# Gathered rows, cumulative sums and a projection: four pairs of tiles stored together, and shorter leads

## The chip, the core and the metric

The kernel runs on one core of a Trainium2 chip. The metric is the device time of one execution in microseconds. The kernel before took 454.2 us in the median of six runs (452.15 to 456.44).

## The reference

For each of 16 batches, 2048 rows of 512 fp32 numbers are picked by sorted indices out of 4096, summed up cumulatively along the rows, and multiplied by a 512 x 512 matrix:

```python
# x: (16, 4096, 512) f32, indices: (16, 2048) i64, w: (512, 512) f32
gathered = x[b_idx, indices, :]
cs = np.cumsum(gathered, axis=1)
return np.matmul(cs, w).astype(np.float32)        # (16, 2048, 512)
```

So 67 MB are read by rows and 67 MB are written.

## The kernel before

The rows are cut into tiles of 128, 16 tiles for a batch and T = 256 in all, and two tiles make a pair (R = 2, G = 128 pairs). Each tile goes through these steps, one function for each, with its line in the profile:

- `gather` (L137, POOL): an indirect DMA brings 128 rows of 2 KB into a buffer `g32`. There are 16 such places (NG), so gather t waits on `s_c` until tile t-16, with its pair, has been cast.
- `cast` (L152, ScalarE): fp32 to fp16, from `g32` to `g16`; where the lead allows, a pair is cast in one instruction of 1024 elements.
- `sums` (L164, PE): four matmuls by a triangle of ones give the cumulative sums within the tile, transposed, into one of four PSUM tiles `pa` (NA).
- `carry` (L196, and L183 for the first tile of a batch, VectorE): adds the last column of the tile before, and writes fp16 `cst`.
- `project` (L208, PE): four matmuls of `cst` with the fp16 weights, into one of four PSUM tiles `pb` (NB).
- `drain` (L220, ScalarE): copies `pb` to a buffer `ob` in SBUF. There are 8 buffers (NO), each holding a pair.
- `store` (L234, SP): one DMA of 512 KB for each pair, 128 partitions of 4 KB, once both tiles of the pair are drained. The first and the last pair (`PLAIN`, L229) are stored as two transfers of 256 KB. Before `ob` is written again, ScalarE waits on `s_o` for the store of eight pairs earlier.

Every engine's order is written out by hand, with semaphores between the engines. ScalarE does, for each u from 0 to 255, the casts listed in `casts[u]` and then the drain of u (`step`). That list lets casts run ahead of the drain by `far` tiles, at most FAR = 10; the lead grows from 2 at the start and shrinks at the end:

```python
far = min(FAR, 2 + u // 4, 2 + (T - 1 - u) // 4)
n = R if far > 4 and len(cast_by) % R == 0 else 1
lead = min(LEAD, 1 + (u + 2) // 4, 1 + (T - 1 - u) // 6)
```

PE's order is made likewise from `lead`: sums run ahead of the projection by at most LEAD = 4 tiles. Inside `sums` and `project` a wait for the next step's buffer stands between the matmuls. PE, VectorE and ScalarE run the middle of their orders as hardware loops over 16 tiles (U); POOL and SP have theirs written out.

Of the kernel before, what the change touches and what calls it, by code (L numbers as in the profile page):

```python
# [7 lines left out]
P = 128  # L8
FP32 = mybir.dt.float32
# [24 lines left out]
def kernel(  # L34
# [7 lines left out]
    nc = tc.nc  # L42

    B, S, D = x.shape
    N = indices.shape[1]
    R = 2
# [3 lines left out]
    T = B * NT  # L50
    G = T // R
# [1 line left out]
    KI = T // P  # L53
    FIRST = 2 * R
    NG = 16
    LEAD = 4
    FAR = 10
    NH = 8
    NA = 4
    NB = 4  # L60
    NC = 4
    NO = 8
    U = NT
    assert U % NG == 0 and U % (R * NO) == 0 and U % NA == 0 and U % (R * NC) == 0 and U % NB == 0
    assert D == 512 and N % (R * P) == 0 and T % P == 0

    x_flat = x.rearrange("b s d -> (b s) d")
# [1 line left out]
    const = ctx.enter_context(tc.tile_pool(name="const", bufs=1))  # L69
# [13 lines left out]
    g32 = [const.tile([P, R, D], FP32, name=f"g32_{i}") for i in range(NG // R)]  # L83
    g16 = [const.tile([P, R, D], FP16, name=f"g16_{i}") for i in range(NH)]
    cst = [const.tile([P, DC, R, P], FP16, name=f"cst{i}") for i in range(NC)]
    ob = [const.tile([P, R, D], FP32, name=f"ob{i}") for i in range(NO)]
    pa = [ps.tile([P, DC, R, Q], FP32, name=f"pa{i}") for i in range(NA)]
    pb = [ps.tile([P, D], FP32, name=f"pb{i}") for i in range(NB)]

# [2 lines left out]
    def sem(name):  # L92
        return tc.alloc_semaphore(name)

    s_z, s_ut, s_wc, s_if, s_pt, s_prep, s_of, s_c = (
        sem(f"s_{n}") for n in ("z", "ut", "wc", "if", "pt", "prep", "of", "c")
    )
    s_first = [sem(f"s_first{k}") for k in range(2)]
    s_w = [sem(f"s_w{c}") for c in range(DC)]
    s_idx = [sem(f"s_idx{k}") for k in range(KI)]  # L100
    s_el = [sem(f"s_el{j}") for j in range(R)]
    s_ol = [sem(f"s_ol{j}") for j in range(R)]
    s_g = [sem(f"s_g{i}") for i in range(NG)]
    s_o = [sem(f"s_o{i}") for i in range(NO)]
    s_a = sem("s_a")
    s_d = sem("s_d")
    s_b = sem("s_b")
    s_e = sem("s_e")

    pool, pe, dve, act, sp = (  # L110
        Lane(e) for e in (nc.gpsimd, nc.tensor, nc.vector, nc.scalar, nc.sync)
    )

    casts = []
    cast_by = []
    for u in range(T):
        far = min(FAR, 2 + u // 4, 2 + (T - 1 - u) // 4)
        casts.append([])
        while len(cast_by) <= min(u + far, T - 1):
            n = R if far > 4 and len(cast_by) % R == 0 else 1  # L120
            casts[u].append((len(cast_by), n))
            cast_by += [cast_by[-1] + 1 if cast_by else 1] * n

    for u in range(3 * U, T - 2 * U):
        assert casts[u] == [(t + U, n) for t, n in casts[u - U]]

    def gather(t):
# [20 lines left out]
    def cast(t, n, first=None):  # L148
        g, r = divmod(t, R)
        for u in range(t, t + n):  # L150
            act.need(s_g[u % NG], 16 * (u // NG + 1), first)
        nc.scalar.copy(  # L152
            out=g16[g % NH][:, r : r + n], in_=g32[g % (NG // R)][:, r : r + n]
        ).then_inc(s_c, 1)
# [62 lines left out]
    def drain(u, first=None):  # L217
        g, j = divmod(u, R)
        act.need(s_b, u + 1, first)
        nc.scalar.copy(out=ob[g % NO][:, j], in_=pb[u % NB][:]).then_inc(s_e, 1)  # L220

    def store(g):
        b, h = divmod(g, GB)
        rows = out[b, h * R * P : (h + 1) * R * P, :]
        if g in PLAIN:
            for j in range(R):
                sp.need(s_e, R * g + j + 1)
                done = s_ol[j] if g else (s_o[0], s_of)[j]
                nc.sync.dma_start(  # L229
                    out=rows[j * P : (j + 1) * P, :], in_=ob[g % NO][:, j]  # L230
                ).then_inc(done, 16)
            return
        sp.need(s_e, R * (g + 1))
        nc.sync.dma_start(  # L234
            out=rows.rearrange("(p j) d -> p j d", j=R), in_=ob[g % NO][:]
        ).then_inc(s_o[g % NO], 16)


    with nc.allow_non_contiguous_dma(reason="a few indices, one per partition"):
        for k, eng in enumerate((nc.sync, nc.scalar)):  # L240
            t = k * R
            eng.dma_start(  # L242
                out=idx_first[:, t : t + R, :],
                in_=indices[0, t * P : (t + R) * P]
# [4 lines left out]
    for k in range(KI):  # L249
        nc.sync.dma_start(  # L250
            out=idx64[:, k, :], in_=idx_rows[k * P : (k + 1) * P, :]
        ).then_inc(s_idx[k], 16)
    for c in range(DC):
        eng = (nc.sync, nc.scalar)[c % 2]
        eng.dma_start(out=w32[:, c, :], in_=w[c * P : (c + 1) * P, :]).then_inc(s_w[c], 16)
    for g in range(G):
        store(g)
    for g in range(G - NO, G - 1):
        sp.need(s_o[g % NO], 16 * (g // NO + 1))
    for j in range(R):  # L260
        sp.need(s_ol[j], 16)


    nc.gpsimd.memset(ident[:], 1.0).then_inc(s_ut, 1)
# [3 lines left out]
        out=ident[:],  # L268
        in_=ident[:],
# [7 lines left out]
        out=ut[:],  # L277
        in_=ut[:],
# [9 lines left out]
        out=uq[:],  # L288
        in_=uq[:],
# [23 lines left out]
    for k in range(KI):  # L313
# [3 lines left out]
            out=pb[k % NB][:, :P], in_=idxf[:, k, :], identity=ident[:]  # L317
# [20 lines left out]
    order = []  # L338
    done = 0
    for u in range(T):  # L340
        lead = min(LEAD, 1 + (u + 2) // 4, 1 + (T - 1 - u) // 6)
        first = u if u // R in PLAIN else u // R * R + R - 1
        while done < T and done <= max(first, u + lead):
            order.append((True, done))
            done += 1
        order.append((False, u))
# [4 lines left out]
    for i in range(head + step, tail):  # L351
        assert order[i] == (order[i - step][0], order[i - step][1] + U)
# [15 lines left out]
    with nc.tensor.Fori(2 * U // R, (T - 2 * U) // R, U // R) as first:  # L368
        pe.new_pass()
        for i in range(head, head + step):  # L370
            run(i, first)
# [7 lines left out]
        act.need(s_w[c], 16)  # L379
        nc.scalar.copy(out=w16[:, c, :], in_=w32[:, c, :]).then_inc(s_wc, 1)  # L380
    def step(u, first=None):
        if u % R == 0:
            if first is None and u == R * NO:
                act.need(s_of, 16)
            act.need(s_o[u // R % NO], 16 * (u // R // NO), first)
        for t, n in casts[u if first is None else 2 * U + u]:
            cast(t if first is None else t - 2 * U, n, first)
        drain(u, first)


    for u in range(2 * U):
        step(u)
    with nc.scalar.Fori(2 * U, T - 2 * U, U) as first:
        act.new_pass()
        for u in range(U):
            step(u, first)
    for u in range(T - 2 * U, T):
        step(u)
# [30 lines left out]
```

## Time and profile before

| | |
|---|---|
| time, median of six runs | 454.2 us |
| the profiled execution: time, span | 457.0 us, 455.3 us |
| PE busy, granted clock | 342.1 us (75%), 0.873 |
| ScalarE (ACT) busy | 260.6 us (57%) |
| POOL busy | 243.7 us (54%) |
| VectorE (DVE) busy | 178.6 us (39%) |
| DMA traffic | 135.69 MB, mean 298 GB/s over the span |
| gathers (L137) | 256, 945 ns of POOL each |
| stores (L234) | 126 of 512 KB |
| drains (L220) | 256, 596 ns mean |
| casts (L152) | 139, 992 ns mean, 117 of them for pairs |
| carries (L196) | 240, 692 ns mean |

How to read it: the page has the share of the span for which each engine was busy, the same in 40 slices, the DMA queues (q0 carries the gathers, q1 the stores and loads that SP issues), and the chain of work that ended last. Beside it there are a list of who waited for whom (total, times, longest), a timeline of the instructions, and tables of any stretch of the span. Starts are counted in us from the start of the span. "remote", and "another core or an unknown queue", is a releaser that the profile doesn't name. Matmuls are pipelined and their ends are modelled, so a busy PE is not PE at its peak.

### The profile page before, as it was taken

The numbers are of one execution on the slowest core, as the hardware profiler recorded it, in microseconds if no ns is written. First come the engines' busy times: TensorE is split into PE (matmuls) and PEld (weight loads), VectorE is DVE, ScalarE is ACT, GpSimd is POOL, SyncE is SP. The second block draws the span as 40 slices with busy tenths as digits, with TensorE's granted clock in tenths as the row PEclk, the third lists the DMA queues.
The fourth block names the chain that finished last, engine by engine and source line by source line (L and its number), as shares of the span: only waits on it lengthen the run. The fifth ranks groups of instructions, "written<-read, shape, count | busy, mean of one in ns | idle before, by whom it ended". The sixth has DMA issues, their size and how long they took to land.

```text
span 455.3 us, 6498 instructions
## 1 busy us (share of the span) xinstructions
PE 342.1 (75%) x2066; PEld 169.8 (37%) x2066; DVE 178.6 (39%) x263; ACT 260.6 (57%) x399; POOL 243.7 (54%) x266
## 2 busy tenths in 40 slices
PE   6127787867868698696987697777876869598895
PEld 2002333433434344343443243334432434244452
DVE  2112333334433345243344444434444434355552
ACT  3104465566655576565566556556666656576684
POOL 6744366575555655565655566556555556565200
PEclk9655689897979978988889799799797999989999
DMA  6846579997889989989988899898888998999974
GB/s 230 256 136 213 180 250 329 331 325 265 309 308 343 321 289 326 328 308 325 335 292 309 300 349 329 296 361 311 302 313 309 303 339 305 325 314 336 348 288 184
DMA packets 40619, 135.69 MB, mean 298 GB/s; under 512 B 6816, under 2 KB 7072, under 8 KB 40608
## 3 DMA queue, kind: packets, MB, share of 16 engines
q0 software_dynamic: 20480, 67.13, 47.4%
q1 hardware_dynamic: 19568, 67.91, 37.3%
q10 hardware_dynamic: 560, 0.53, 0.3%
q8 instruction: 5, 0.08, 0.1%
q14 instruction: 6, 0.05, 0.0%
HBM read 68.42 MB, written 67.11 MB: 298 GB/s over the span
## 4 chain that ended last, share of the span: by engine, by line
PE 67%; another core or an unknown queue 14%; issue 8%; DVE 5%; ACT 4%; DMA 1%; SPq 0%; DVEq 0%; ACTq 0%
PE pb L208 49%; PE pa L164 17%; DVE cst L196 4%; ACT g L152 2%; ACT ob L220 2%; DVE cst L183 1%; DMA idx<-in_indices_dram 1%; PE pb L304 0%; SPq L250 0%; SPq L242 0%; PE pb L316 0%; DVE idxf L311 0%; DVEq L26 0%; DVEq L328 0%
## 5 line engine op out<-in xcount | busy, mean ns | idle before, releaser
L137 POOL DMA_INDIRECT g<-in_x_dram,idxg x252 | 238.2, 945 | 178.9 <-ACT g L152 114.3
L208 PE MATMUL pb<-w,cst 128*128 128x512 f16 x1024 | 299.7, 417 | 44.3 <-DVE cst L196 30.0
L196 DVE TENSOR_TENSOR cst<-pa,cst 128x512 f16<-128x512 f32 x240 | 166.1, 692 | 244.3 <-PE pa L164 157.1
L220 ACT COPY ob<-pb 128x512 f32<-128x512 f32 x256 | 145.3, 596 | 184.9 <-PE pb L208 107.0
L164 PE MATMUL pa<-ut,g 128*128 128x128 f16 x1008 | 112.6, 234 | 60.3 <-issue 37.4
L208 PEld LDWEIGHTS pb<-w,cst 128*128 128x128 f16 x1024 | 94.5, 106 | 130.4 <-DVE cst L196 41.8
L152 ACT CAST g<-g 128x1024 f16<-128x1024 f32 (+1 forms) x139 | 137.7, 992 | 0.9 <-DMA g<-in_x_dram,idx_first 0.9
L164 PEld LDWEIGHTS pa<-ut,g 128*128 128x128 f16 x1008 | 81.5, 105 | 141.7 <-issue 65.0
L183 DVE CAST cst<-pa 128x512 f16<-128x512 f32 x16 | 11.0, 688 | 20.1 <-PE pa L164 15.1
L304 PE MATMUL pb<-zeros 128*128 128x512 f16 x16 | 5.4, 498 | 1.5 <-DVE zeros L308 1.5
L137 POOL DMA_INDIRECT g<-in_x_dram,idx_first x4 | 4.0, 994 | 1.6 <-issue 0.9
L304 PEld LDWEIGHTS pb<-zeros 128*128 128x128 f16 x16 | 1.9, 126 | 4.0 <-issue 1.9
L164 PE MATMUL pa<-uq,g 128*128 128x128 f16 x16 | 1.6, 220 | 2.3 <-issue 2.1
L377 ACT ACT_TABLE_LOAD x1 | 1.3, 1283 | 2.5 <-issue 2.5
L380 ACT CAST w<-w 128x512 f16<-128x512 f32 x2 | 1.1, 616 | 2.6 <-DMA w<-in_w_dram 2.6
L164 PEld LDWEIGHTS pa<-uq,g 128*128 128x128 f16 x16 | 1.0, 97 | 3.6 <-issue 2.7
L311 DVE CAST idxf<-idx 128x128 f32<-128x128 uint32 x2 | 0.5, 266 | 3.7 <-DMA idx<-in_indices_dram 3.7
L325 DVE CAST w<-w 128x512 f16<-128x512 f32 x2 | 0.8, 435 | 1.7 <-DMA w<-in_w_dram 1.7
L316 PE MATMUL pb<-ident,idxf 128*128 128x128 f32 x2 | 0.6, 301 | 0.4 <-DVE idxf L311 0.4
L308 DVE MEMSET zeros<- 128x256 uint32 x1 | 0.3, 272 | 1.1 <-SPq L90 1.1
L322 DVE CAST idxg<-pb 128x128 uint32<-128x128 f32 x2 | 0.6, 288 | 0.3 <-PE pb L316 0.3
L316 PEld LDWEIGHTS pb<-ident,idxf 128*128 128x128 f32 x2 | 0.3, 140 | 0.9 <-DVE idxf L311 0.7
(11 smaller groups left out, 2.1 us busy)
## 6 DMA issues: line engine op xcount, KB each, us to landing
out_dram<-ob SPq DMA_DIRECT2D x126, 512.0 KB
g<-in_x_dram,idxg POOLq DMA_INDIRECT x252
out_dram<-ob SPq DMA_DIRECT2D x4, 256.0 KB, 2.0
w<-in_w_dram ACTq DMA_DIRECT2D x2, 256.0 KB
w<-in_w_dram SPq DMA_DIRECT2D x2, 256.0 KB
idx<-in_indices_dram SPq DMA_DIRECT2D x2, 128.0 KB, 2.8
g<-in_x_dram,idx_first POOLq DMA_INDIRECT x4
idx_first<-in_indices_dram ACTq DMA_DIRECT2D x1, 2.0 KB, 2.1
```

The lines of the kernel that those rows point to most:

```text
L137: nc.gpsimd.indirect_dma_start(out=g32[g % (NG // R)][:, r, :], out_offset=None, in_=x_flat, in_offset=bass.IndirectOffsetOnAxis(ap=ap, ax ...
L152: nc.scalar.copy(out=g16[g % NH][:, r : r + n], in_=g32[g % (NG // R)][:, r : r + n]).then_inc(s_c, 1)
L164: mm = nc.tensor.matmul(out=pa[t % NA][:, c], lhsT=g16[g % NH][:, r, c * P : (c + 1) * P], rhs=uq[:] if first is None and g in PLAIN else ...
L183: nc.vector.tensor_copy(out=dst, in_=src).then_inc(s_d, 1)
L196: nc.vector.tensor_tensor(out=dst, in0=src, in1=last, op=mybir.AluOpType.add).then_inc(s_d, 1)
L208: mm = nc.tensor.matmul(out=pb[u % NB][:], lhsT=cst[g % NC][:, c, j, :], rhs=w16[:, c, :], start=(c == 0), stop=(c == DC - 1),)
L220: nc.scalar.copy(out=ob[g % NO][:, j], in_=pb[u % NB][:]).then_inc(s_e, 1)
L304: nc.tensor.matmul(out=pb[NB - 1][:], lhsT=zeros[:, :P], rhs=zeros[:], start=True, stop=True)
L316: nc.tensor.transpose(out=pb[k % NB][:, :P], in_=idxf[:, k, :], identity=ident[:]).then_inc(s_pt, 1)
L325: nc.vector.tensor_copy(out=w16[:, c, :], in_=w32[:, c, :]).then_inc(s_wc, 1)
L377: nc.scalar.copy(out=spare[:], in_=zeros[:, :1])
L380: nc.scalar.copy(out=w16[:, c, :], in_=w32[:, c, :]).then_inc(s_wc, 1)
```

## The change

- Four pairs are kept in one buffer `ob` (W = 4; four such buffers, NO = 4, so 32 tiles where there were 16) and stored together once all eight tiles are drained: as H = 4 transfers, each of 32 partitions with four pieces of 4 KB, 512 KB each. The first four and the last four pairs are still stored pair by pair.
- ScalarE waits for the store of a buffer once in eight tiles instead of once in two; its loop now covers 32 tiles (V) instead of 16.
- Casts run ahead of the drain by at most 6 tiles instead of 10 (FAR), with another growth at the start (4 from tile 2 on, 5 from 12, 6 from 28) and another decrease at the end. Pairs are cast in one instruction only at the full lead, so there are 154 casts.
- Sums run ahead of the projection by at most 3 tiles instead of 4 (LEAD), by 2 from tile 2 on and by 3 from tile 16.

```diff
-    LEAD = 4
-    FAR = 10
+    LEAD = 3
+    FAR = 6
-    NO = 8
+    W = 4
+    H = 4
+    NO = 4
     U = NT
+    V = max(U, W * R * NO)
...
-    ob = [const.tile([P, R, D], FP32, name=f"ob{i}") for i in range(NO)]
+    ob = [const.tile([P, W, R, D], FP32, name=f"ob{i}") for i in range(NO)]
...
-        far = min(FAR, 2 + u // 4, 2 + (T - 1 - u) // 4)
+        far = min(FAR, 2 if u < 2 else 4 + (u + 4) // 16, 3 + (T - 1 - u) // 8)
...
-            n = R if far > 4 and len(cast_by) % R == 0 else 1
+            n = R if far > 5 and len(cast_by) % R == 0 else 1
...
-        nc.scalar.copy(out=ob[g % NO][:, j], in_=pb[u % NB][:]).then_inc(s_e, 1)
+        nc.scalar.copy(out=ob[g // W % NO][:, g % W, j], in_=pb[u % NB][:]).then_inc(s_e, 1)
 
-    def store(g):
+    def store(g, n):
         b, h = divmod(g, GB)
-        rows = out[b, h * R * P : (h + 1) * R * P, :]
+        rows = out[b, h * R * P : (h + n) * R * P, :]
+        src = ob[g // W % NO]
...
-        sp.need(s_e, R * (g + 1))
-        nc.sync.dma_start(
-            out=rows.rearrange("(p j) d -> p j d", j=R), in_=ob[g % NO][:]
-        ).then_inc(s_o[g % NO], 16)
+        sp.need(s_e, R * (g + n))
+        rows = rows.rearrange("(g p j) d -> p g j d", p=P, j=R)
+        src = src[:, g % W : g % W + n]
+        if n < W:
+            done = s_ol if g >= W else (s_o[0], s_of)[R + g > H]
+            nc.sync.dma_start(out=rows, in_=src).then_inc(done, 16)
+            return
+        for i in range(H):
+            part = slice(i * P // H, (i + 1) * P // H)
+            nc.sync.dma_start(out=rows[part], in_=src[part]).then_inc(s_o[g // W % NO], 16)
...
-    for g in range(G):
-        store(g)
...
+    for g in range(W):
+        store(g, 1)
+    for g in range(W, G - W, W):
+        store(g, W)
+    for g in range(G - W, G):
+        store(g, 1)
...
-        lead = min(LEAD, 1 + (u + 2) // 4, 1 + (T - 1 - u) // 6)
+        lead = min(LEAD, 1 if u < 2 else 2 + u // 16, (T - 1 - u) // 2)
...
     def step(u, first=None):
-        if u % R == 0:
-            if first is None and u == R * NO:
-                act.need(s_of, 16)
-            act.need(s_o[u // R % NO], 16 * (u // R // NO), first)
+        if first is None and u == min(W * R * NO, 2 * U - 1):
+            act.need(s_of, 16 * (R + W - 1 - H))
+        if u % (W * R) == 0:
+            stored = first if first is None else first * (16 * H) // (R * W * NO)
+            act.need(s_o[u // R // W % NO], 16 * H * (u // R // W // NO), stored)
...
-    with nc.scalar.Fori(2 * U, T - 2 * U, U) as first:
+    with nc.scalar.Fori(2 * U, T - 2 * U, V) as first:
```

## The prediction, made before the changed kernel was run

> **What bounds the kernel now.** I read the page's slices first, because they tell whether one limit holds all the way.
>
> ```profile
> PEclk9655689897979978988889799799797999989999
> DMA  6846579997889989989988899898888998999974
> ```
>
> Three stages show. From slice 2 to slice 5 (some 23 to 68 us) the DMA engines are half used; to slice 37 they are at 8 to 9 tenths; then they empty. The windows give numbers for the head, the middle and the end.
>
> ```profile
> core 0: us, PE busy (x) PEld busy (x) DVE busy (x) ACT busy (x) POOL busy (x), PEclk, DMA share, GB/s
> 20.00:62.00 42.00, 22.98 (x96) 10.03 (x97) 9.69 (x14) 12.58 (x23) 19.48 (x21) 0.58 0.60 193
> 62.00:417.00 355.00, 278.33 (x1718) 139.82 (x1717) 146.36 (x213) 214.58 (x322) 204.15 (x216) 0.89 0.90 316
> 425.00:440.00 15.00, 13.64 (x95) 7.02 (x94) 8.90 (x13) 13.03 (x21) 0.16 (x1) 1.00 0.81 320
> ```
>
> In the middle no compute engine is full (PE 78%, ScalarE 60%), and the DMA engines are at 0.90: that stage is within a tenth of their limit. Counting the drains (L220) in the timeline, tile 16 is drained at 67.7 us and tile 224 at 416.2: 1.68 us a tile. POOL issues a gather every 1.25 us while it is free, so the rest is waiting, and the list of waits names it.
>
> ```profile
> POOL g L137 <- ACT g L152: 114.3, 41, 4.9
> ACT ob L220 <- remote: 69.5, 26, 13.7
> DVE cst L196 <- remote: 62.5, 19, 7.1
> ```
>
> POOL waits for casts to free gather buffers; ScalarE stands in order behind a drain; VectorE and ScalarE wait for a signal whose sender the profile doesn't name. In the POOL timeline this is a rhythm: eight gathers (243.4 to 253.2 us), then 3.65 us of idleness, then the next eight. Casts wait for nothing but the two first gathers (0.9 us in all): data always lie ready, and it is buffers coming free that are late.
>
> The head has a different limit, which the chain of waits shows.
>
> ```profile
> 17.91 13.67 another core or an unknown queue
> ...
> 44.27 0.58 ACT ob L220
> 44.85 0.53 ACT g L152
> 45.38 0.05 issue
> 45.42 0.61 PE pa L164 x4
> 46.03 1.72 PE pb L208 x4
> 47.75 0.02 issue
> 47.78 0.58 ACT ob L220
> ```
>
> Drain, cast, sums, projection, drain: one serial ring of 3.5 us, since before tile 12 the cast that the next sums need stands behind the drain of the projection before them. The drains of tiles 2 to 12 lie at 31.6 and 61.9 us, 3.0 us a tile, at half the PE clock (a projection takes 1.72 us here and 0.86 us at the end).
>
> Last, the queues:
>
> ```profile
> q0 software_dynamic: 20480, 67.13, 47.4%
> q1 hardware_dynamic: 19568, 67.91, 37.3%
> ```
>
> By these shares 4 KB of gather cost 0.474 x 455.3 x 16 us / 16,389 = 211 ns of an engine, and 4 KB of store 164 ns. In the end stage, where only stores are left, slices of the DMA view between 440 and 456 us reach 420 GB/s, with all 128 partitions in each store.
>
> **The change, part by part.** The sum is made against the profiled execution: 457.0 us for a span of 455.3; the median of six is 454.2, so 2.8 us come off at the end. A measurement of this kernel can tell about 0.5% (2.3 us) from no change.
>
> *Head schedules.* Casts run four tiles ahead from tile 2 on, where they ran two to four; sums lead by two from tile 2 on. Tiles 4, 5 and 6 are cast before drain 2, so sums of 5 no longer wait for drain 2, and so on down the ring. Each link sheds drain, cast and gaps: 0.58 + 0.53 + 0.07 = 1.18 us. The chain between 31.6 and 62 us has eight such links: 9.4 us. Against it, casts of 4 and 5 ahead of drain 2 free two more gathers (20 and 21), and if the long wait at 17.9 us lasts as long as POOL issues without a pause, as it seems to (POOL stops at 28.1, the drain comes at 31.6), it grows by 2 x 1.25 = 2.5 us. Net gain 7; bounds 0 (the gathers then become the limit, although at 0.60 of the DMA engines there is room for 0.30 x 42 = 13 us) and 13.
>
> *Cast form.* Single casts go on to tile 33, so there are 154 instead of 139. Fifteen pairs (1.05 us) become thirty singles (0.62): 15 x 0.19 = 2.9 us more on ScalarE, which is idle for 29 of the 42 us where they fall. Nothing; 2.9 if that cover were gone.
>
> *Leads in the middle.* Casts 6 instead of 10 ahead of the drain, sums 3 instead of 4. Gather t waits for the cast of t-16 with either lead; only ScalarE's place in its own order moves, by four tiles. Between two pauses POOL is freed as many buffers as ScalarE casts, so the rhythm should stay: zero. PE stops when its four projection tiles are full, that is at projection u+3 with drain u pending. It then needs sums u+6, hence cast u+6, which is just done. If that just fails, each of some 28 rhythms in the middle pays one cast and sums, 0.53 + 0.05 + 0.61 = 1.2 us: 33 us. No instruction is added to PE or VectorE.
>
> *Drain buffers.* 32 tiles where there were 16. Waits for a store have no row of their own; some of the 69.5 us under "remote" could be such, and a larger ring could only shorten them. Nothing tells how many, so zero. ScalarE's loop goes round 6 times and not 12; no row prices a turn, zero.
>
> *Stores.* SP issues four transfers for eight tiles before and after (332 ns each), 30 groups of 2.1 MB. SP waits for eight drains where it waited for two, and nobody else queues there. What changes is timing and shape: no store work for some 13 us, then 2.1 MB at once, in pieces that touch 32 partitions. The trace has no such store. Lower bound: a full queue fills holes in the middle's DMA time, of which 0.10 x 355 = 35 us exist; the whole of it is not to be had, since the rhythm's pauses leave gathers short. Upper bound by the nearest row: stores cost what gathers cost, 211 ns in place of 164: 15,360 packets x 47 / 16 = 45 us, less what the 35 us of holes take up. The bytes, the 4 KB pieces and the queue stay as they were, so I take the store row itself: zero. That is the weak step of this sum.
>
> The Trainium skill speaks against this part. "SBUF — State Buffer", section on the DMA port swizzle, says that partitions 0 to 31 reach 8 of the 16 ports, with 189 GB/s measured for them and 328 GB/s for all 128. By that page each group would need 11.1 us and not 6.4: as an estimate 30 x 4.7 = 141 us more if nothing hid it. "DMA: Bandwidth & Descriptors", rules for kernel authors, also says not to split a transfer by partitions. The before trace shows no store of fewer than 128 partitions, so it can't say whether this holds beside gathers.
>
> *End.* At the last gather (424.2 us) 231 tiles are drained. With the new leads gather 255 waits for a cast that stands at step 234 instead of 230, so four tiles fewer follow: 4 x 1.09 = 4.4 us. Their stores move ahead of the last gather: 1.05 MB at 316 GB/s, 3.3 us if the DMA engines set the pace there. And the last 2.1 MB group is issued when tile 247 is drained (441.1 us), followed by 2.1 MB of single pairs: 4.2 MB at 410 GB/s, 10.2 us, as long as the drains of 248 to 255 last (to 451.0). Gain 1; bounds -3 and +4.
>
> Sum: 457.0 - 7 - 1 = 449; by the median 446 us.
>
> **The rivals.**
>
> *Narrow stores cost more (slower).* Four 32-partition pieces behind each other crowd the same places while gathers run. At the gather row's price, 45 us, with half of the holes (18) as cover: 446 + 27 = 473 us; with the whole of them 456, with none 491. It decides from a mean store packet of about 191 ns: 27 ns more x 15,360 / 16 = 26 us, which is the half cover and the 8 us gained. For: DMA at 0.90, no slack beyond a tenth. Against: stores at 164 ns next to gathers at 211 show no crowding today.
>
> *Shorter leads bind (slower).* The 33 us above, at once visible as PE waiting for casts: 446 + 33 = 479 us. For: the margin is exact, not ample. Against: PE is only 78% busy and POOL's pause outlasts the delay.
>
> *Bursts fill the holes (faster still).* Half of 35 us: 446 - 18 = 428 us.
>
> *The head's gain is given back.* The middle stage starts earlier but has the same bytes to move, so buffers are late at tile 16 instead: 454 us.
>
> **How the numbers follow.** Forecast 0.40, deeper gain 0.10, given back 0.08, narrow stores 0.32, leads 0.10. Faster by over 0.5%: 0.50; within: 0.08; slower: 0.42. Cases of both signs hold the chance; the forecast's own range is 438 to 452. The range over all is 430 to 482: below lie the deeper gain's better half, above a quarter of the narrow stores and half of the leads, together under 2 in 10.
>
> **What would show it.** Right: the chain between 30 and 60 us loses its cast links, drain 12 comes by 55 us, about 1.68 us a tile stays, the store queue keeps 164 ns per 4 KB. Wrong: q1's share well above 37%, with 190 ns or more per 4 KB; PE sums waiting for L154's casts in every rhythm; a POOL pause longer than 3.65 us; drains of the last eight tiles waiting on nothing while stores still run for more than 4 us.

## The result, and the profile after

The changed kernel takes 454.6 us in the median of 34 runs (450.43 to 459.65), the kernel before 454.58 in 71 runs beside it (449.69 to 458.24). The ratio is 0.9994, 95% interval 0.9973 to 1.0015: no change, where 446 us was forecast. A ratio compares, within one series of runs on one chip, only the runs of each kernel that lie within 1.5% of its fastest, so it need not be the quotient of the medians; the profiled execution of the kernel before, 457.0 us, lies just above that.

The profiled execution of the changed kernel took 454.68 us, span 453.0, granted clock 0.903. The slices of its page:

```profile
DMA  7866689999999999999999999999999999999997
GB/s 230 251 190 200 219 237 348 309 329 299 307 307 344 300 340 347 315 337 310 253 318 326 320 356 309 343 324 307 310 333 332 341 323 293 310 299 345 268 221 233
```

The DMA engines were at 8 to 9 tenths in the middle; now they show nine from slice 6 to the last but one, and in the middle still move about 320 GB/s. In the last three slices, the first two of them at nine tenths as well, they move only 221 to 268 GB/s. The windows give numbers:

```profile
core 0: us, PE busy (x) PEld busy (x) DVE busy (x) ACT busy (x) POOL busy (x), PEclk, DMA share, GB/s
20.00:62.00 42.00, 25.98 (x144) 13.43 (x143) 12.46 (x18) 18.28 (x34) 24.06 (x26) 0.75 0.68 209
62.00:417.00 355.00, 267.00 (x1727) 140.96 (x1726) 149.05 (x217) 217.68 (x331) 204.13 (x216) 0.92 0.98 319
425.00:440.00 15.00, 12.91 (x82) 5.66 (x81) 6.73 (x10) 11.61 (x23) 0.00 (x0) 1.00 0.97 226
```

Read the last two columns. The head has more work done in the same 42 us (POOL 24.06 us instead of 19.48). In the middle the share goes from 0.90 to 0.98 for the same rate. In the end stage the share is 0.97 (0.81 before) and the rate 226 GB/s (320 before): full engines that move little.

The queues say which transfers do that:

```profile
q1 hardware_dynamic: 19568, 67.91, 52.6%
q0 software_dynamic: 20480, 67.13, 40.7%
```

By the prediction's own formula 4 KB of store now cost 0.526 x 453.0 x 16 us / 16,579 = 230 ns of an engine (164 before), 4 KB of gather 0.407 x 453.0 x 16 / 16,389 = 180 ns (211 before).

The chain of waits between 25 and 43 us (start, length, what):

```profile
25.34 9.77 another core or an unknown queue
...
38.19 1.71 PE pb L210 x4
39.90 0.43 PE pa L166 x4
40.33 1.25 PE pb L210 x4
41.57 0.22 PE pa L166 x4
41.80 0.86 PE pb L210 x4
```

The ring of drain, cast, sums and projection is gone: between 36 and 45 us the chain is PE alone, projection and sums in turn. Counted in the timeline, drain 2 comes at 31.6 us as before, drain 12 at 51.6 (61.9 before), gather 32 at 50.6 (59.8), gather 64 at 103.8 (109.8), the last gather at 418.3 (424.2). In this pair of profiles a third of the head's gain is gone by gather 64.

The three waits that the prediction named are still there:

```profile
POOL g L139 <- ACT g L154: 102.2, 43, 4.5
DVE cst L198 <- remote: 62.7, 22, 9.9
ACT ob L222 <- remote: 58.4, 19, 13.3
```

POOL still waits for casts (102.2 us in all, 114.3 before), and VectorE and ScalarE still wait for a signal from an unnamed sender. POOL's pauses, mostly 3.6 us before, are now between 1 and 3.7 us, often 3.2 and 1.8. From gather 64 to gather 240 the pace is 1.649 us a gather (1.654 before). So the middle did not notice that its stores became dearer.

The end did. The rates in the DMA view of 425 to 453 us, 0.7 us a column:

```profile
GB/s 345 310 222 199 199 199 181 345 304 199 222 199 170 187 234 205 211 217 187 205 193 275 293 205 205 187 199 205 257 375 427 404 421 386 401 184 56 3 0 0
```

About 200 GB/s as long as 32-partition pieces are left, then 375 to 427 for the last pairs, which go out over all 128 partitions. The last drain lies 8.3 us ahead of the end (4.3 before), the last gather 34.7 us (31.1 before). Sum for the two executions: 5.9 us gained up to the last gather, 3.6 lost after it, 2.3 left (span 455.3 to 453.0). The medians of many runs leave nothing: the profiled execution of the kernel before lies 2.4 us above its median, that of the changed kernel at its own.

### The profile page after: what moved, and what is told of

Same layout as the page of the kernel before. It is cut to its first block, busy times and chain, and to the rows that moved or that the text cites. A ratio compares the mean times of both kernels' runs of the same rounds, so it can differ in the third digit from the quotient of the medians.

```text
span 453.0 us, 6445 instructions
## 1 busy us (share of the span) xinstructions
PE 328.3 (72%) x2066; PEld 170.2 (38%) x2066; DVE 178.7 (39%) x263; ACT 264.2 (58%) x414; POOL 244.5 (54%) x266
## 4 chain that ended last, share of the span: by engine, by line
PE 65%; another core or an unknown queue 10%; DVE 10%; issue 9%; ACT 2%; DMA 1%; POOL 0%; DVEq 0%; SPq 0%; ACTq 0%
PE pb L210 48%; PE pa L166 17%; DVE cst L198 10%; ACT ob L222 1%; DMA g<-in_x_dram,idx_first 1%; ACT g L154 1%; DMA idx_first<-in_indices_dram 0%; DVE cst L185 0%; POOL g L139 0%; DVEq L26 0%; ACTq L26 0%; SPq L436 0%; SPq L93 0%
## 5 line engine op out<-in xcount | busy, mean ns | idle before, releaser
L210 PE MATMUL pb<-w,cst 128*128 128x512 f16 x1024 | 290.5, 410 | 102.3 <-DVE cst L198 84.4
L139 POOL DMA_INDIRECT g<-in_x_dram,idxg x252 | 239.0, 948 | 172.2 <-ACT g L154 102.2
L154 ACT CAST g<-g 128x1024 f16<-128x1024 f32 (+1 forms) x154 | 140.0, 912 | 0.8 <-DMA g<-in_x_dram,idx_first 0.6
L166 PE MATMUL pa<-ut,g 128*128 128x128 f16 x1008 | 104.8, 230 | 11.0 <-issue 7.1
```

The costliest lines, as they stand in the source:

```text
L139: nc.gpsimd.indirect_dma_start(out=g32[g % (NG // R)][:, r, :], out_offset=None, in_=x_flat, in_offset=bass.IndirectOffsetOnAxis(ap=ap, ax ...
L154: nc.scalar.copy(out=g16[g % NH][:, r : r + n], in_=g32[g % (NG // R)][:, r : r + n]).then_inc(s_c, 1)
L166: mm = nc.tensor.matmul(out=pa[t % NA][:, c], lhsT=g16[g % NH][:, r, c * P : (c + 1) * P], rhs=uq[:] if first is None and g in PLAIN else ...
L210: mm = nc.tensor.matmul(out=pb[u % NB][:], lhsT=cst[g % NC][:, c, j, :], rhs=w16[:, c, :], start=(c == 0), stop=(c == DC - 1),)
```

## The experiments

Theory: the head gains what its ring shed, and the 32-partition pieces give it back at the end, where nothing covers them. Rivals: the grouping itself (waiting for eight drains, then a burst) costs; the shorter leads cost; the head's gain never reaches the end.

One thing is needed to read the numbers. The experiments ran in six series. The kernel before took 447.8 us in the first, 445.5 in the fourth and 446.1 in the sixth, but 353.1 in the second, third and fifth; every series lay wholly on one side, and all comparisons of times are within a series. I call them series near 450 and series near 353. Some of the texts on record say "this call" for a series, and some put the difference down to the chip.

The texts of the first series reckon from 454.2 us, and its kernel before took 447.8. So they are to be read as differences, and a time that falls into one of their ranges bears out nothing by itself.

**Parts of the change, series near 450** (kernel before 447.82 us, 440.5 to 453.63).

`wide_group`: the changed kernel, its four pieces cut by pairs and not by partitions.

```diff
-            part = slice(i * P // H, (i + 1) * P // H)
-            nc.sync.dma_start(out=rows[part], in_=src[part]).then_inc(s_o[g // W % NO], 16)
+            nc.sync.dma_start(out=rows[:, i], in_=src[:, i]).then_inc(s_o[g // W % NO], 16)
```

> The changed kernel, with the four transfers of a group cut by pairs (128 partitions of 4 KB each) and not by partitions; bytes, sizes, count and moment of issue stay. Theory N (transfers of 32 partitions run at half rate when nothing but stores is left, and the end pays for it): 4 KB of store back to about 164 ns, the end from the last gather 7 to 9 us shorter, 445 to 448 us. Rival B (it is the bursts of 2.1 MB that cost, whatever their shape): the end stays, 453 to 456 us.

Measured: 445.76 us, ratio to before 1.0047 (1.0003 to 1.009). Theory N asked for 6 to 9 us less than the kernel before; there are 2.1 by the medians and none by the ratio, so the total doesn't bear it out. The end does: in its profile the last gather is 28.6 us ahead of the end (34.7 in the changed kernel), the last drain 4.3 (8.3), and 4 KB of store cost 0.406 x 439.2 x 16 / 16,579 = 172 ns.

`leads_only`: the kernel before with the new FAR, LEAD and schedules.

```diff
-    LEAD = 4
-    FAR = 10
+    LEAD = 3
+    FAR = 6
...
-        far = min(FAR, 2 + u // 4, 2 + (T - 1 - u) // 4)
+        far = min(FAR, 2 if u < 2 else 4 + (u + 4) // 16, 3 + (T - 1 - u) // 8)
...
-            n = R if far > 4 and len(cast_by) % R == 0 else 1
+            n = R if far > 5 and len(cast_by) % R == 0 else 1
...
-        lead = min(LEAD, 1 + (u + 2) // 4, 1 + (T - 1 - u) // 6)
+        lead = min(LEAD, 1 if u < 2 else 2 + u // 16, (T - 1 - u) // 2)
```

> The kernel before, with the changed leads and cast schedule; stores stay pair by pair, 128 partitions. Theory N: the head's 8 us and the four tiles fewer at the end are kept, 444 to 448 us. Rival G (what the head gains is given back in the middle, since the bytes are the same): 452 to 456 us.

Measured: 444.7 us, ratio 1.0012 (0.9961 to 1.0063). Shorter leads do not bind: a price of 33 us is excluded. That they gain, 6 to 10 us by the text, is not shown here: 3.1 us by the medians, but the interval of the ratio holds 1.

`stores_only`: the reverse of that diff in the changed kernel, so new stores with the old schedules.

> The changed kernel, with the leads and cast schedule of the kernel before: only the stores are changed. Theory N: the head as before, the end some 5 to 9 us longer, 459 to 464 us, with 4 KB of store at about 230 ns and of gather at about 180 ns. Rival G: within 2 us of before, 453 to 456 us.

Measured: 452.38 us, ratio 1.0208 (1.0133 to 1.0283), 4.6 us above the kernel before by the medians and 7.7 above `leads_only`, which differs in the leads as well. 4 KB of store cost 221 ns and of gather 184, close to the text. In the profiles the middle runs at 1.620 us a gather (1.615 in `leads_only`), and the last gather is 37.6 us ahead of the end (30.2 there; 29.1 in `head_only` below, which ends with the same leads as `stores_only`). So most of the loss lies behind the last gather: 7.4 or 8.5 us, by the profile that it is held against.

`head_only`: the kernel before, with longer leads at the start and nothing else.

```diff
-        far = min(FAR, 2 + u // 4, 2 + (T - 1 - u) // 4)
+        far = min(FAR, max(2 + u // 4, 2 if u < 2 else 4 + (u + 4) // 16), 2 + (T - 1 - u) // 4)
...
-        lead = min(LEAD, 1 + (u + 2) // 4, 1 + (T - 1 - u) // 6)
+        lead = min(LEAD, 1 if u < 2 else max(2, 1 + (u + 2) // 4), 1 + (T - 1 - u) // 6)
```

> The kernel before, with the changed growth of both leads at the start alone (four tiles from tile 2 on; sums two ahead); the limits of 10 and 4 and the decrease at the end stay. If the head ring was worth 8 us to the end: 445 to 448 us. Rival G: 452 to 456 us, with tile 32 early and tile 224 at its old time.

Measured: 444.11 us, ratio 0.9919 (0.9843 to 0.9995): 3.7 us off by the medians, where 6 to 9 were asked, and the interval just misses 1. That speaks, weakly, against the rival that gives the head's gain back in the middle.

The ten profiles near 450, those of the later series among them, say it more firmly. Gather 32 is issued at 54.8 to 59.8 us in the four with the old schedules and at 50.5 to 52.1 in the six with the new ones; gather 64 at 102.8 to 109.8 and 99.3 to 103.8. From the last gather to the end it takes 32.7 to 37.6 us in the three with 32-partition pieces at the end and 28.6 to 31.1 in the other seven.

**The stores by themselves.** `stores_alone` issues nothing but stores: four parts of 16.8 MB, as four pair transfers over 128 partitions, four of 32 partitions, two of 64, and one of 2 MB.

```diff
...
+            if k == 0:
+                pieces = [(rows[:, i], src[:, i]) for i in range(4)]
+            elif k == 1:
+                pieces = [(rows[i * 32 : (i + 1) * 32], src[i * 32 : (i + 1) * 32]) for i in range(4)]
+            elif k == 2:
+                pieces = [(rows[i * 64 : (i + 1) * 64], src[i * 64 : (i + 1) * 64]) for i in range(2)]
+            else:
+                pieces = [(rows, src[:])]
...
```

> Everything but the stores is left out, and the buffers hold ones: 4 x 8 groups of 2.1 MB, 16.8 MB a part, one part after another: four transfers of one pair over 128 partitions; four of 32 partitions; two of 64; one of all. Theory N: 400 to 420 GB/s in the first and last part and half of it, 200 to 220, in the second (84 us and not 41 us), with packets of 159 and about 320 ns. If shape cost nothing by itself: four equal parts of about 41 us.

The DMA view of its whole span (5.7 us a column):

```profile
GB/s 0 0 0 269 406 402 404 409 404 406 276 225 234 256 268 243 274 248 273 265 248 271 129 223 232 271 317 367 396 414 408 266 232 405 404 404 402 408 409 286
```

The four parts are plain: a plateau at 404, one at about 255, a rise from 225 to 410, and 404 again. By their ends in the timeline they took 41.6 us (404 GB/s), 66.9 (251), 53.4 (314) and 41.6 (403). A mean packet took 164 ns in the first and 252 ns in the second, where a tenth took 159 or less and a tenth 322 or more. Cutting by pairs costs nothing against one 2 MB transfer; cutting by partitions does. The page "SBUF — State Buffer" of the Trainium skill, section on the DMA port swizzle, gave 189 against 328 GB/s, a ratio of 0.58; here it is 251 against 404, or 0.62, so for 32 partitions the rule holds, and its rate is lower than that of four pieces queued behind each other.

**A series near 353.** `after_again` is the changed kernel as it is, `before_again` a profile of the kernel before.

> The changed kernel once more, beside the variants of this call. Theory N (the head's gain of some 4 to 6 us is eaten by stores at half rate in the end): 0 to 2 us from the kernel before, and the last gather 4 to 7 us earlier than before's with an end some 4 to 8 us longer. Rival G (the gain is lost in the middle): the last gather at before's time.

> The kernel before, for its profile beside those of the variants. Both theories: tile 32's gather issued at 56 to 60 us, the last gather to the end 30 to 31 us.

Measured: 375.67 us against 353.06, ratio 1.0535 (1.0474 to 1.0596). The changed kernel is clearly slower here, which neither text foresaw; times that the texts name for 450 do not apply. The windows and then the list of waits of `before_again` show what the middle is when it runs freely:

```profile
62.00:330.00 268.00, 244.37 (x1690) 126.19 (x1689) 145.31 (x210) 211.00 (x316) 197.60 (x209) 1.00 1.03 414
```

```profile
POOL g L137 <- issue: 71.9, 236, 0.3
ACT g L152 <- DMA g<-in_x_dram,idxg: 55.9, 94, 1.4
```

POOL issues a gather every 1.25 us, with 0.3 us of idleness between two, and no pause. Casts wait for gathers (55.9 us; 0.9 us in the first profile). No wait for an unnamed sender is in the list; the clock is 1.00, the DMA engines are full at 414 GB/s. There is no hole to hide anything in. The waits of `after_again`, then the store queue of `after_again` and of `before_again`:

```profile
POOL g L139 <- ACT g L154: 33.3, 53, 2.2
ACT g L154 <- DMA g<-in_x_dram,idxg: 90.2, 107, 3.6
```

```profile
q1 hardware_dynamic: 19568, 67.91, 50.7%
q1 hardware_dynamic: 19568, 67.91, 47.9%
```

Gathers land later (90.2 us of waiting instead of 55.9; 69.6 in `wide_group_2` below, which has the same leads and wide pieces), casts come later, and POOL is held up by them for 33.3 us. By the formula 4 KB of store cost 0.507 x 375.1 x 16 / 16,579 = 184 ns, and 162 in `before_again`: 22 x 15,360 / 16 = 21 us of DMA time in stages that have none to spare. The last gather moves from 322.3 to 339.5 us (17.2 us, at 1.33 us a gather), and what follows it grows from 29.2 to 35.6 us (6.4): together the 23.6 us by which the span grows (351.5 to 375.1). This execution, 376.8 us, is one of the longer ones of six (370.24 to 381.17); the ratio makes the loss 19 us.

`wide_tail`: the changed kernel, its last five groups cut by pairs.

```diff
-            nc.sync.dma_start(out=rows[part], in_=src[part]).then_inc(s_o[g // W % NO], 16)
+            piece = (rows[:, i], src[:, i]) if g >= G - 6 * W else (rows[part], src[part])
+            nc.sync.dma_start(out=piece[0], in_=piece[1]).then_inc(s_o[g // W % NO], 16)
```

> The changed kernel with the pieces of the last five groups alone cut by pairs, 128 partitions each; 25 groups before them stay in pieces of 32 partitions. Theory N: narrow stores cost only where nothing hides them, so all of the loss goes, 4 to 8 us under the changed kernel, equal to the variant with wide pieces throughout. Rival M (narrow stores cost in the middle too): less than half of that.

Measured: 368.61 us, ratio to before 1.0422 (1.0365 to 1.0478): 4 us under `after_again` by the ratios, 7 by the medians. Most of the loss stays, so here rival M holds: narrow stores cost in the middle too. The five groups begin at tile 208, and in the profiles half of what they save lies ahead of the last gather (334.8 us instead of 339.5) and half behind it (31.0 us instead of 35.6).

**The parts again, another series near 353** (kernel before 353.11 us).

> All pieces 128 partitions wide, groups and leads as in the changed kernel. On a chip where the kernel before runs near 353 us: theory N (narrow pieces cost in the middle and the end) 353 to 358 us, gathers 1.25 us apart in the middle; rival L (the shorter leads leave too little in hand) 362 to 368 us with gathers 1.30 us apart. On a chip where it runs near 450 us: 1 to 4 us under the kernel before.

> Stores of the kernel before, leads of the changed one. Near 353 us: theory N, at or a little under the kernel before (head 3 us earlier, POOL's 1.25 us a gather rules after it); rival L, 362 to 368 us. Near 450 us: 2 to 4 us under.

> Stores of the changed kernel, leads of the one before. Near 353 us: theory N, 368 to 376 us, of which 6 to 8 us in the end; rival L, at most 360 us. Near 450 us: 4 to 6 us over.

> The kernel before with the changed growth of the leads at the start. Near 353 us: 0 to 3 us under, since POOL issues without a pause from the start and the head is hidden behind it. Near 450 us: 3 to 5 us under.

| kernel | us | ratio to before |
|---|---|---|
| `wide_group_2` | 352.63 | 0.9986 (0.9962 to 1.001) |
| `leads_only_2` | 351.76 | 0.9965 (0.9946 to 0.9984) |
| `stores_only_2` | 380.29 | 1.077 (1.0726 to 1.0813) |
| `head_only_2` | 352.53 | 0.9988 (0.9973 to 1.0003) |

The same grouping with 128 partitions costs nothing against the kernel before (`wide_group_2`), and with 32 it costs 27 us with the old leads (`stores_only_2`, above the 368 to 376 us of its text) and 19 to 23 with the new (`after_again`). So it is the shape of the pieces, not the wait for eight drains and not the burst. The head's gain is not seen here: POOL's 1.25 us sets the pace from the start, and gather 64 lies at 83.5 us in `before_again` and `after_again` alike. `leads_only_2` is the one version whose interval lies below 1 near 353, by 0.35%.

**The end alone, near 450** (fourth series; kernel before 445.48 us, 436.77 to 449.97). `wide_tail_2` is the kernel of `wide_tail`, `after_3` the changed kernel beside it.

> The changed kernel with the last five groups of eight tiles cut by pairs into four 128-partition transfers; the other groups stay narrow. My theory for a chip where the kernel before takes about 450 us: the narrow stores cost only at the end, so this takes all of it away: 3 to 5 us less than the changed kernel, 1 % less than the kernel before. The rival, narrow stores also cost in the middle there: under 2 us less than the changed kernel. On a chip where the kernel before takes 353 us: 368, as already measured on one.

> The changed kernel once more, as the partner of wide_tail_2 on this chip. Where the kernel before takes about 450 us: a ratio of 0.995 to 1.005. Where it takes 353 us: 375 us, ratio 1.05.

Measured: 443.92 us (443.39 to 445.7) and 446.46 us (444.67 to 448.5), six runs each; only one run of `after_3` (444.67) lies below the highest of `wide_tail_2`. The 2.5 us are a little under my 3 to 5 and above the rival's 2; the 1 % under the kernel before was a miss (0.4 % by the medians). The DMA view of 413 to 442 us in `wide_tail_2`:

```profile
GB/s 424 407 345 339 254 0 85 407 407 407 401 412 401 373 23 0 0 0 0 130 390 413 401 396 412 390 418 418 396 412 164 260 412 353 59 133 229 0 0 0
```

Bursts at 400 GB/s with empty columns between them: the stores wait for drains again. In the profiles the last drain lies 4.2 us ahead of the end (8.1 in `after_3`), while the middle, still narrow, keeps its pace (1.615 and 1.606 us a gather). With five of thirty groups widened, the end's price is gone: 28.6 us from the last gather, 32.7 in `after_3`.

**What keeps the middle slow near 450.** Where the middle is slow, the narrow stores cost it nothing, so I tried three reductions of the kernel before.

`thin_stores`:

```diff
-            out=rows.rearrange("(p j) d -> p j d", j=R), in_=ob[g % NO][:]
+            out=rows.rearrange("(p j) d -> p j d", j=R)[0 : P // 8], in_=ob[g % NO][0 : P // 8]
```

> The kernel before, in which each of the 126 pair stores moves only its first 16 partitions: seven eighths of the output of these pairs are left out, all gathers and all computing stay. It asks what makes the signals of the middle late where the kernel takes about 450 us. If the load on the DMA engines makes them late, the middle goes to POOL's own 1.25 us a gather, the idle time put down to an unnamed releaser goes, and the time is near 350 us. If the gathers themselves do it, the pauses stay and the time stays above 420 us. On a chip where the kernel before takes 353 us it says only what the gathers alone need: 345 to 350 us.

Measured in the fourth series: 439.29 us in one run (kernel before 445.48). Its window of the middle, its waits and the queue of its gathers:

```profile
62.00:417.00 355.00, 282.26 (x1795) 143.35 (x1794) 154.13 (x224) 221.84 (x337) 206.82 (x219) 0.93 0.64 184
```

```profile
POOL g L137 <- ACT g L152: 94.8, 36, 5.6
DVE cst L196 <- remote: 47.9, 20, 11.9
ACT ob L220 <- remote: 45.3, 17, 6.6
```

```profile
q0 software_dynamic: 20480, 67.13, 53.5%
```

With the DMA engines at 0.64 POOL still pauses, for long stretches 3.4 to 3.5 us after every eight gathers, at 1.593 us a gather, and the unnamed sender stays. With hardly any stores beside them 4 KB of gather cost 0.535 x 437.5 x 16 / 16,389 = 229 ns, more than in any other profile here. The load on the DMA engines does not set the pace.

`half_project` and `half_project_2` (one kernel), `half_gathers`:

```diff
+            half = first is not None or 2 * U <= u < T - 2 * U
+            if half and c % 2:
+                continue
...
-                stop=(c == DC - 1),
+                stop=(c == (DC - 2 if half else DC - 1)),
...
+        n = P // 2 if 2 * NG <= t < T - 2 * NG else P
+        ap = ap[0:n]
...
-            out=g32[g % (NG // R)][:, r, :],
+            out=g32[g % (NG // R)][0:n, r, :],
```

> The kernel before, in which the projections of tiles 32 to 223 do two of their four matmuls; the other half of each of these products is left out, all else stays, gathers, stores and signals too. It asks whether PE's own load makes its signals late in the middle, on a chip where the kernel before takes about 450 us. If PE's load does it, POOL's pauses of 3.5 us go, the middle runs at 1.25 us a gather, and the time is near 360 us. If the gathers do it, the pauses stay: above 420 us. Where the kernel before takes 353 us, it stays there.

> The kernel before, in which the gathers of tiles 32 to 223 bring 64 rows instead of 128; the other half of these rows is left out, all else stays, the number of gathers too. On a chip where the kernel before takes about 450 us: if the gathers make PE's signals late, less of them makes the pauses shorter or rarer, and the middle goes towards PE's own 1.1 us a tile: 330 to 400 us. If PE's load makes them late, nothing changes: above 420 us. Where the kernel before takes 353 us: PE's own pace, 320 to 345 us.

> The kernel of half_project once more (the projections of tiles 32 to 223 leave out two of their four matmuls), for a chip where the kernel before takes about 450 us; the run of half_project fell on one where it takes 353. If PE's load makes its signals late: POOL's pauses go and the time is near 360 us. If not: above 420 us, with pauses of 3 us and more. Where the kernel before takes 353 us, 353 again.

The first two fell into a series near 353 (kernel before 353.14), one run each: 353.56 us with half of the middle's projections, which agrees with PE not setting the pace there, and 335.8 us with half of the gathered rows. `half_project_2` ran near 450: 438.35 us in one run against 446.06. Its window and its waits:

```profile
62.00:417.00 355.00, 237.43 (x1426) 122.52 (x1424) 155.44 (x226) 224.25 (x340) 208.31 (x220) 0.76 0.91 331
```

```profile
POOL g L137 <- ACT g L152: 92.7, 35, 5.5
DVE cst L196 <- remote: 84.7, 29, 10.5
ACT ob L223 <- remote: 79.9, 29, 9.5
```

A fifth fewer matmuls in the whole kernel, a granted clock of 0.76 instead of 0.89, and much the same pauses (mostly 3.5 to 3.9 us) at 1.584 us a gather. PE's own load does not set the pace either. And this series ran on the very chip on which the third series had the kernel before at 353.11 us, so my texts were wrong to put the difference down to the chip. What delays these signals stays open: the gathers themselves were only reduced near 353, so they are neither shown nor excluded.

## Why the prediction was wrong, point by point

**Head schedules (+7).** The mechanism was right: the cast links left the chain, drain 12 came at 51.6 us where "by 55" was the sign. From drain 2 to drain 12 the ring shed 10.3 us (9.4 reckoned), and the 2.5 us against it did not come: drain 2 stayed at 31.6. Of this 9.2 us were there at gather 32, but only 6.0 at gather 64 and 5.9 at the last gather, in one pair of profiles; `head_only` gives 3.7 by the medians. So +7 was too large. What takes a part back between gathers 32 and 64 is not shown.

**Cast form, leads in the middle, drain buffers (0 each).** Right within what was measured. `leads_only` contains the first two and is not slower in either kind of series. `wide_group` adds the larger ring and the grouping to it and lies 1.1 and 0.9 us above it. The rival in which the leads bind is out, and its sign is missing: the weight loads of the sums waited 9.9 us for casts in all, 27.9 before.

**Stores (0): the step that failed.** The trace had no 32-partition store, and I took the row of 128-partition stores, 164 ns, for it. It is 230 ns in the changed kernel and 252 ns alone. That is (230 - 164) x 15,360 / 16 = 63 us of DMA time, more than the 45 us of my upper bound, and near 450 it reached the time only at the end, with 28.6 us from the last gather in wide pieces and 34.7 in narrow ones.

Why it cost the middle nothing near 450 is the second half of the error. I read a share of 0.90 as "within a tenth of their limit" and counted 35 us of holes. The traces show otherwise: the middle of the kernel before moved 316 GB/s at 0.90 in one execution and 414 at 1.03 in another (`before_again`), and kept its slow pace at 0.64 (`thin_stores`). So the DMA engines did not set that pace, and a longer packet there is not a longer kernel. By the shares the 63 us went into two places: the gathers' packets got shorter, (211 - 180) x 16,389 / 16 = 32 us, and the share rose, 0.08 x 355 = 28 us. Why the gathers' packets got shorter is not shown; that they wait behind stores does not fit `thin_stores`, where they took 229 ns with an eighth of the bytes stored. Near 353 the DMA engines are full, and 19 (`after_again`, by the ratio) to 27 us (`stores_only_2`) came through.

**End (+1).** It measured -3.6 in the profile, just past its lower bound of -3. The term reckoned 4.2 MB at 410 GB/s "as long as the drains"; but the group just ahead of the last pairs goes at 200 GB/s, and the pairs queue behind it on SP. The sign that the prediction named, last stores running more than 4 us past the last drain, is there with 8.3 us. `wide_tail_2` takes it away. With wide pieces the same leads end 28.6 us after the last gather (`wide_group`, `wide_tail_2`), 2.5 less than the 31.1 before, so it is the pieces and not the leads that turned the sign.

So of the 8 us that were forecast, in these two profiles 4.6 are missing at the end (-3.6 instead of +1) and 1.1 in the head (5.9 instead of 7); the 2.3 that are left are no more than the 2.4 by which the profiled execution of the kernel before lies above its median. With runs of the kernel before between 440.5 and 453.6 us in one series, the parts can't be told apart more finely near 450.

**The rivals.** "Narrow stores cost more" had the mechanism, and its case with the whole of the holes as cover, 456 us, is close to the time. Its decision point, 191 ns, was passed (230) without the price of 26 us, since it took time of DMA packets for time of the kernel, and it looked for the loss in the middle instead of where the gathers have ended. Near 353, where the DMA engines are full, the loss does lie mostly ahead of the last gather (17.2 of 23.6 us). "The head's gain is given back" has the time, 454 us, but the cause at best in part: a third of the gain is gone by gather 64, the larger loss comes at the end. "Bursts fill the holes" did not happen: the share rose by slower packets, at an unchanged pace.

## What to carry to other kernels

Alone, stores that touch a quarter of the partitions each took 66.9 us where full ones took 41.6, even with four of them queued one behind another; cut a large store along the free dimension. A high share of the DMA engines says neither how much they move nor that they set the pace: read it together with the GB/s. And a packet's time is no price: 230 ns near 450 cost the middle nothing, 184 ns near 353 cost it 17 us. So price a change of shape where the DMA engines set the pace, here in a full middle and at the end. A gain in the head and a loss at the end can sum to an unchanged median; here the old stores with longer leads at the start are what may be left to take (`head_only`, 0.8 % near 450 with an interval that just misses 1, and nothing shown near 353; `leads_only`, 0.35 % near 353).

## What was not expected of the hardware

- The same kernel took 353 us in some series and 446 to 454 in others, on one chip once 353.11 and once 446.06. The difference is mostly in the middle: 1.25 or 1.65 us a gather, the latter with POOL's pauses of some 3.5 us and with waits for signals from an unnamed sender. Neither storing only an eighth of the bytes nor leaving out half of the projections' matmuls removed them.
- 64 partitions are between 32 and 128: 314 GB/s, against 251 and 404, in transfers of 1 MB, and within that part the rate rose from 223 to 414.
- Fewer matmuls did not raise the granted clock: 0.76 in the middle of `half_project_2`, 0.89 in that of the kernel before.
